# Issuing each dense group of one sequence's projection behind a given matmul of the other's attention

## The chip, the cores and the metric

The kernel runs on one core of a Trainium2 chip. A core has a matrix engine (TensorE, PE in the profile, with its weight loads as PEld), a vector engine (DVE), a scalar engine (ACT), GpSimd (POOL), a synchronisation engine (SP) that here only issues DMAs, and 16 DMA engines. Each engine runs its own program in order; between engines there are semaphores. The metric is the device time of one execution in microseconds.

## The reference

One layer of an encoder is applied, with the same weights, to two sequences: the *prompt* (1024 tokens, number 0 in the code) and the *sample* (512 tokens, number 1), each with 16 learned tokens ahead. The widths are 1024, 64 per head, and 2816 in the feed-forward part.

```python
n = rms_norm(x, g_mix)
proj = n @ w_in                                   # qa ka va | qb kb vb, 18 blocks of 128 columns
qa, ka = rope(rms_norm(qa)), rope(rms_norm(ka))   # group A: 8 query heads, 2 key heads
oa = softmax(qa ka^T * scale) va
qb, kb = rope(qb), rope(kb)                       # group B: 4 heads with two maps each
p = softmax(qb kb^T * scale)
ob = rms_norm((p[0] - lam * p[1]) vb)
h = x + concat(oa, ob) @ w_out
m = rms_norm(h)
h = h + (gelu(conv3(m @ w_gate)) * (m @ w_up)) @ w_down
y = rms_norm(h)[16:]
```

## The kernel before

**Numbers.** Products of float32 are made from two rounded halves of each operand, `hi` and `lo`. `split` (L122) makes them, and `mm3` (L129 to 133) adds three matmuls: hi with hi (L131), lo with hi (L132), hi with lo (L133). `dense` (L136) does this for the eight blocks of 128 input channels, so a *dense group*, one tile of 128 output columns by up to 384 tokens, is 24 matmuls. `load_weight` (L144) fetches a weight tile on ACT's DMA queue and splits it.

**Stages.** `trunk_kernel` (L857) first runs the projection of the sample. Then it runs the attention of the sample together with the projection of the prompt; then the attention of the prompt together with all that is left of the sample (output projection and feed-forward); then the rest of the prompt.

**The projection of the prompt** (`projection`, L165) is a generator. It has three token chunks of 384, 384 and 272 for each weight tile. `keys_a` (L301) does the keys of group A, `values` (L333) a tile of values, with transposes at L346, and `pair` (L277) two tiles of queries or keys, with a normalisation matmul at L257 in group A, the rotation on DVE (L292, L294), the sum on POOL (L297) and stores to DRAM on SP (L272). The order is keys A, values A, queries A, values B, queries A, values B, then the keys, queries and values of B in turn. After each dense group it yields its cost, `24 * cw` in `pair` and `25 * cw` in the other two, cw being the number of tokens: 455,520 in sum. What follows a group (normalisation, transposes, stores) is traced when the generator goes on, in one step with the next group.

**The attention** (`attention`, L391) is a generator too. It loads keys and queries (L414) and values (L434), all on SP. `softmax` (L439) makes the scores of up to 128 queries into `ps_s` (L446, L447; two chunks of keys for the sample, three for the prompt), evicts them on DVE (L450), which gives ps_s free for the next, and exponentiates on ACT (L453). There is one buffer of ps_s. `weighted_v` (L456) transposes the probabilities on PE (L467) into ps_t (two buffers), splits them on ACT and DVE, and multiplies by the values into ps_o (L477 to L482); the last part, 16 keys, is L491. A head of group A is four softmaxes (for the sample; the prompt does that twice, as two blocks), a transpose of the reciprocal sums (L500) and a weighted V. After each four heads of A a small *halo* of 8 queries follows. A head of group B is two blocks for the sample, of two and three query tiles with two softmaxes each. The yielded costs add up to 211,728 for the sample: 15,488 for each head of A, 176 for a halo and 21,868 for a head of B. In the prompt a block of A is 29,824.

**What sets the order.** `merge` (L823) draws from the two generators in turn, by the costs passed so far. This is the order of tracing and the priority in the scheduler, which lays out each engine's program from modelled times: an instruction that is ready may come ahead of one traced earlier that isn't. `tc.issue_after(ins)` adds an edge to every instruction traced inside it on the engine of `ins`: it is placed behind `ins` in that engine's program. For an edge within one engine there is no semaphore.

In the first call, `LEAD1` lets the projection go 20,000 units ahead, and `R1` has it traced at 1.1 units per unit of attention; when the attention is through, `merge` ends, and the rest of the projection is traced by `drain` (L843). `HOLD` places the first four steps of the attention behind the dense group traced before them. In the second call `LEAD2` lets the prompt's attention go 120,000 units ahead, four blocks, and HOLD places the first four steps of the sample's output projection behind the last matmul of weighted V traced by then.

**Memory.** The projection's and the attention's tiles of the prompt lie on the same side of SBUF, one after the other: the prompt's attention gets its tiles as those of the projection are released. PSUM's ps_s, ps_t and ps_o are opened anew for the prompt's attention, in the banks that the sample's held.

```python
        with ExitStack() as es1:
            merge(g, attention(es1, g, 1, "right"), R1[0], p0, R1[1], LEAD1, HOLD)
        drain(p0)
```

Of the kernel before, what the change touches and what calls it, by code (L numbers as in the profile page):

```python
# [21 lines left out]
P = 128  # L22
# [99 lines left out]
def split(g, hi, lo, src, lo_engine=None):  # L122

    nc = g.nc
    return (nc.scalar.copy(hi, src),  # L125
            (lo_engine or nc.vector).tensor_tensor(out=lo, in0=src, in1=hi.bitcast(F32), op=ALU.subtract))  # L126
# [264 lines left out]
def attention(ctx, g, s, side):  # L391
    nc, tc = g.nc, g.tc
# [23 lines left out]
    def load_q(j, maps, c0, cw):  # L416
        out = []
        for first in range(2):
            q = qp.tile([P, max(514, 2 * max(sum(m for _, m in b) for b in blocks))], F32R, name="q", tag=f"q{first}")
            for i, m in enumerate(maps):  # L420
                stacked(q[:, i * cw:(i + 1) * cw], j, m, first, c0, cw)
            out.append(q)
        return out
# [8 lines left out]
    def load_v(i, w, c0):  # L432
        v = vp.tile([P, nf * 2 * P], F32R, name="v", tag="v")[:, :nf * w].rearrange("p (t c) -> p t c", c=w)
        nc.sync.dma_start(out=v.bitcast(F32), in_=g.v[s][0][:, c0 // P] if i == 0 else g.v[s][i])  # L434
        tail = vp.tile([P, P], F32R, name="v_tail", tag="v_tail")[:64 if i == 0 else 96]
        nc.sync.dma_start(out=tail.bitcast(F32), in_=g.vt[s][i][:tail.shape[0], c0:c0 + P])
        return v, tail

    def softmax(q, k, l):  # L439

        M = q[0].shape[-1]
        p = pp.tile([P, ne], F32, name="p", tag="p")[:M]
        ps = g.psum.wide(M, nch, kw)
        for i in range(nch):
            kc = k[:, i * kw:(i + 1) * kw]
            nc.tensor.matmul(ps[:, i], lhsT=q[0], rhs=kc, start=True, stop=False)  # L446
            nc.tensor.matmul(ps[:, i], lhsT=q[1], rhs=kc, start=False, stop=True)  # L447

        nm = sp.tile([P, 1], F32, name="nm", tag="nm")[:M]
        g.evicted = nc.vector.tensor_scalar(out=p.rearrange("p (i w) -> p i w", i=nch), in0=ps, scalar1=-HD ** -0.5,  # L450
                                            scalar2=3.0e38, op0=ALU.mult, op1=ALU.min, accum_out=nm).ins
        p = p[:, :n]
        nc.scalar.activation(p, p, AF.Exp, bias=nm, scale=-1.0, accum_out=l)  # L453
        return p

    def weighted_v(pl, v, diff):  # L456

        W = sum(p.shape[0] for p in pl)
        o = g.psum.tile(P, W, "o")
        v, v_tail = v  # L460

        def transposed(k0, kw):
            tps = g.psum.tile(kw, W, "t")
            c = 0
            for p in pl:
                M = p.shape[0]
                nc.tensor.transpose(tps[:, c:c + M], p[:, k0:k0 + kw], g.ident[:M, :M])  # L467
                c += M
            return tps

        for i in range(nf):
            tps = transposed(i * P, P)
            hi = ptp.tile([P, 512], F32R, name="pt_hi", tag="pt_hi")[:, :W]
            lo = ptp.tile([P, 512], F32R, name="pt_lo", tag="pt_lo")[:, :W]
            split(g, hi, lo, tps)
            if diff:
                nc.tensor.matmul(o, lhsT=v[:, i, 0:P], rhs=hi, start=i == 0, stop=False)  # L477
                nc.tensor.matmul(o, lhsT=v[:, i, P:2 * P], rhs=hi, start=False, stop=False)  # L478
                nc.tensor.matmul(o, lhsT=v[:, i, 0:P], rhs=lo, start=False, stop=False)  # L479
            else:  # L480
                nc.tensor.matmul(o, lhsT=v[:, i, :], rhs=hi, start=i == 0, stop=False)  # L481
                nc.tensor.matmul(o, lhsT=v[:, i, :], rhs=lo, start=False, stop=False)  # L482
            yield 5 * W

        tps = transposed(n - 32, 32)
        parts = ptp.tile([P, 512], F32R, name="pt_hi", tag="pt_hi")[:, :W]
        g.marks = [i.ins for i in split(g, parts[0:32], parts[32:64], tps)]
        if diff:
            nc.scalar.copy(parts[64:96], tps)
        rows = v_tail.shape[0]  # L490
        g.mark = nc.tensor.matmul(o, lhsT=v_tail, rhs=parts[:rows], start=False, stop=True).ins  # L491
        yield 2 * W
        return o, W

# [35 lines left out]
    for kv in range(2):  # L530
        k = load_k(KA, kv)
        v = load_v(0, P, kv * P)
        halo = [sp.tile([P, 8], F32R, name="halo", tag=f"halo{f}", bufs=2) for f in range(2)]
        for i in range(4):
            h = kv * 4 + i
            for b in range(nblk):
                q = load_q(QA + 2 * kv, [i], NMETA + 512 * b - 2, 514)
                load_r()
                pl = []
                l = sp.tile([P, 4], F32, name="l_a", tag="l_a", bufs=3)  # L540
                for t in range(4):
                    pl.append(softmax([x[:, 2 + t * P:2 + (t + 1) * P] for x in q], k, l[:, t:t + 1]))
                    if t == 1 and b == 0:
                        with tc.issue_after(g.evicted):
                            for f in range(2):
                                nc.vector.tensor_copy(halo[f][:, 2 * i:2 * i + 2], q[f][:, 0:2])
                    yield 2 * n
                cols = slice(1 + 512 * b, 513 + 512 * b)
                reciprocals(l, g.rT[s][h, cols].rearrange("(t p) -> t p", p=P))
                o, W = yield from weighted_v(pl, v, False)  # L550
                oa = finish_a(o, W)
                store_a()
                late.append((oa, g.rT[s][h:h + 1, cols], g.oT[s][h * HD:(h + 1) * HD, cols]))
        l = sp.tile([P, 4], F32, name="l_a", tag="l_a", bufs=3)[:8, 0:1]
        load_r()
        p = softmax(halo, k, l)
        r = sp.tile([P, 4], F32, name="r_a", tag="r_a", bufs=3)[:8, 0:1]
        nc.vector.reciprocal(out=r, in_=l)
        nc.scalar.activation(p, p, AF.Copy, scale=r)
        o, W = yield from weighted_v([p], v, False)  # L560
# [34 lines left out]
    for h in range(4):  # L595
        ks = [load_k(KB + h // 2 * 2, h % 2 * 2 + m) for m in range(2)]
        v = load_v(1 + h, 2 * P, 0)
        rows = g.oT[s][512 + h * P:512 + (h + 1) * P]
        for blk in blocks:
            c0 = blk[0][0]  # L600
            W = sum(m for _, m in blk)
            q = load_q(QB + h // 2 * 2, [h % 2 * 2 + m for m in range(2)], c0, W)
# [3 lines left out]
            lead = 1 if c0 < NMETA else 0  # L606
# [213 lines left out]
        yield 4 * cw  # L820


def merge(g, a, wa, b, wb, lead, hold):  # L823

    done = [0.0, lead]
    after, held = None, 0
    while True:
        i = 0 if b is None or done[0] / wa <= done[1] / wb else 1
        if i == (lead > 0) and held < hold:
            after, held = after or g.mark, held + 1  # L830
            order = g.tc.issue_after(after)
        else:
            order = nullcontext()
        try:
            with order:
                done[i] += next((a, b)[i])
        except StopIteration:
            if i == 0:
                break
            b = None  # L840


def drain(gen):  # L843
    for _ in gen:
        pass
# [5 lines left out]
NRAW, NW = 2, 3  # L851
R1, R2 = (1.0, 1.1), (1.0, 1.0)
LEAD1, LEAD2, HOLD, STATS = -20000.0, 120000.0, 4, 26


@with_exitstack
def trunk_kernel(ctx, tc, g):  # L857
    nc = tc.nc
# [73 lines left out]
    with ExitStack() as es0:  # L932
        p0 = projection(es0, g, 0, "left", "mm", "mm")
        with ExitStack() as es:
            zero = zp.tile([16, 2 * P], F32, name="zero")
            nc.vector.memset(zero, 0.0)
            g.zero = zp.tile([16, 2 * P], F32R, name="zero_r")
            nc.vector.tensor_copy(g.zero, zero)
            p1 = projection(es, g, 1, "right", "p", "t")
            for _ in range(STATS):  # L940
                next(p1)
            next(p0)
            drain(p1)
        zes.close()
        g.psum.relay(s=1, t=2, o=1)
        with ExitStack() as es1:
            merge(g, attention(es1, g, 1, "right"), R1[0], p0, R1[1], LEAD1, HOLD)
        drain(p0)
    g.psum.close()
    g.psum = Psum(tc, "psb", mm=2)  # L950
# [1 line left out]
    with ExitStack() as es1:  # L952
        st1 = state(es1, 1, "right", True)

        def sample():
            yield from mixer_out(g, 1, st1, "right", True, "mm")
            yield from conv_glu(es1, g, 1, st1, "right", 1)
        f1 = sample()
        with ExitStack() as es0:
            merge(g, attention(es0, g, 0, "left"), R2[0], f1, R2[1], LEAD2, HOLD)  # L960
        drain(f1)
        g.psum.relay(s=3)
        st0 = state(ctx, 0, "left", False)
        drain(mixer_out(g, 0, st0, "left", False, "s"))
# [69 lines left out]
```

## Time and profile before

| | |
|---|---|
| time, median of 3 runs | 2184.26 us |
| lowest and highest | 2183.82 and 2185.66 us |
| the profiled execution's own time | 2184.81 us |
| its span, first to last instruction | 2182.7 us |
| mean granted TensorE clock | 0.989 |
| PE busy | 2114.2 us (97%) |
| DVE busy | 1319.2 us (60%) |
| ACT busy | 1024.9 us (47%) |
| POOL busy | 624.0 us (29%) |

The profile is that of one execution. Matmuls overlap in the engine's pipeline, so one lasts longer than it holds up the next: the pace is read from the starts. A row of the timeline is start, duration (both in us), engine, line, operation, what it writes and reads, its size, how many were merged into the row, and in brackets the idle time of that engine ahead of it with what ended it. A row of the windows view is a stretch of time, its length, then the busy time with the number of instructions, the granted clock of PE, the mean busy share of the DMA engines and the GB/s that they moved. Some matmul records, a few per cent, can be missing.

### The profile page before, as it was taken

The page shows a single profiled execution, that of the slowest core. Times are in us where ns is not written, and L with a number is a line of the kernel's source. Part 1 is how long each engine was busy: PE and PEld are TensorE (multiplying, and loading weights), DVE is VectorE, ACT ScalarE, POOL GpSimd, SP SyncE. Part 2 cuts the span into 40 slices and gives each one's busy share as a digit, 9 for nine tenths or more (in the row PEclk, how much of TensorE's full clock was granted, in tenths as well). Part 3 has the DMA queues.
Part 4 walks back from the last instruction along what each step waited for, and adds up shares of the span by engine and source line. Part 5 has one row for each costly group of instructions (what it writes and reads, how often), then busy time and mean ns, then how long its engine had stood idle before and what let it go on. Part 6 is the DMA issues. An engine that isn't in the chain of part 4 may idle for free.

```text
span 2182.7 us, 32285 instructions
## 1 busy us (share of the span) xinstructions
PE 2114.2 (97%) x12442; PEld 1899.7 (87%) x12442; DVE 1319.2 (60%) x2288; ACT 1024.9 (47%) x1803; POOL 624.0 (29%) x465
## 2 busy tenths in 40 slices
PE   8999999988999999999999998999999999999997
PEld 7889999986897888898889898988888888888886
DVE  7645565777767667677777766754434344443346
ACT  6434545667756444677777645542121222112224
POOL 5763444310123222344454314530011100111004
PEclk9999999989999999999999999999999999999999
DMA  6663445563233223232332126511111111111112
GB/s 237 214 218 110 149 156 172 162 209 93 76 94 90 88 68 92 90 108 96 110 111 88 65 88 213 183 68 47 41 49 39 58 49 49 44 34 58 49 39 78
DMA packets 112137, 222.77 MB, mean 102 GB/s; under 512 B 14064, under 2 KB 65520, under 8 KB 111472
## 3 DMA queue, kind: packets, MB, share of 16 engines
q1 hardware_dynamic: 83184, 115.84, 16.7%
q10 hardware_dynamic: 28800, 104.87, 14.7%
q8 instruction: 98, 1.61, 0.3%
q14 instruction: 55, 0.45, 0.1%
HBM read 172.11 MB, written 48.55 MB: 101 GB/s over the span
## 4 chain that ended last, share of the span: by engine, by line
PE 82%; DVE 8%; ACT 3%; issue 3%; DMA 2%; POOL 1%; SPq 0%; ACTq 0%; DVEq 0%; POOLq 0%
PE ps_mm L131 20%; PE ps_mm L132 20%; PE ps_mm L133 20%; PE ps_t L467 5%; PE ps_s L446 4%; PE ps_s L447 3%; PE ps_o L482 2%; DVE p L450 1%; PE ps_o L481 1%; PE ps_o L479 1%; DVE w_lo L126 1%; PE ps_o L477 1%; PE ps_o L478 1%; DVE y L797 1%; DVE pt_lo L126 1%
## 5 line engine op out<-in xcount | busy, mean ns | idle before, releaser
L131 PE MATMUL ps_mm<-xhi,w_hi 128*128 128x512 f32 (+6 forms) x2112 | 703.4, 334 | 2.6 <-DVE hn L117 2.5
L133 PE MATMUL ps_mm<-xhi,w_lo 128*128 128x512 f32 (+6 forms) x2112 | 698.1, 331 | 0.0
L132 PE MATMUL ps_mm<-xlo,w_hi 128*128 128x512 f32 (+6 forms) x2112 | 697.9, 331 | 0.0
L131 PEld LDWEIGHTS ps_mm<-xhi,w_hi 128*128 128x128 f32 x2112 | 400.0, 190 | 28.4 <-DVE hn L117 3.1
L132 PEld LDWEIGHTS ps_mm<-xlo,w_hi 128*128 128x128 f32 x2112 | 399.4, 189 | 25.0 <-issue 0.5
L133 PEld LDWEIGHTS ps_mm<-xhi,w_lo 128*128 128x128 f32 x2112 | 399.2, 189 | 24.4 <-issue 0.5
L125 ACT CAST w_hi<-w_f 128x1024 fp32r<-128x1024 f32 x134 | 139.2, 1047 | 389.9 <-PE ps_mm L132 359.4
L126 POOL TENSOR_TENSOR a_lo<-gate,a_hi 128x512 fp32r<-128x512 f32 x66 | 100.7, 1525 | 651.8 <-ACT a_hi L125 651.6
L450 DVE TENSOR_SCALAR_CACHE_REDUCE p<-ps_s 128x1044 f32<-128x1044 f32 (+7 forms) x212 | 223.3, 1053 | 92.8 <-PE ps_s L447 77.1
L125 ACT CAST pt_hi<-ps_t 128x512 fp32r<-128x512 f32 (+8 forms) x360 | 171.0, 484 | 197.2 <-PE ps_t L467 180.3
L771 DVE TENSOR_TENSOR h<-ps_mm,h 128x512 f32<-128x512 f32 (+1 forms) x288 | 182.3, 645 | 123.7 <-PE ps_mm L133 122.8
L453 ACT ACTIVATE p<-p,nm 128x1040 f32<-128x1040 f32 (+7 forms) x212 | 215.3, 1016 | 85.2 <-DVE p L450 84.4
L126 DVE TENSOR_TENSOR pt_lo<-ps_t,pt_hi 128x512 fp32r<-128x512 f32 (+6 forms) x312 | 173.1, 564 | 102.4 <-ACT pt_hi L125 101.4
L131 PE MATMUL ps_mm<-a_hi,w_hi 128*128 128x512 f32 (+1 forms) x576 | 214.6, 384 | 1.2 <-ACT a_hi L125 1.2
L132 PE MATMUL ps_mm<-a_lo,w_hi 128*128 128x512 f32 (+1 forms) x576 | 215.3, 377 | 0.0
L133 PE MATMUL ps_mm<-a_hi,w_lo 128*128 128x512 f32 (+1 forms) x576 | 215.0, 376 | 0.0
L446 PE MATMUL ps_s<-k,q 128*128 128x348 f32 (+6 forms) x552 | 180.2, 332 | 16.5 <-DVE p L450 16.1
L467 PE MATMUL ps_t<-ident,p 128*128 128x128 f32 (+10 forms) x1188 | 183.8, 269 | 0.3 <-ACT r_rows L502 0.3
L447 PE MATMUL ps_s<-k,q 128*128 128x348 f32 (+6 forms) x552 | 173.7, 320 | 0.0
L126 DVE TENSOR_TENSOR w_lo<-w_f,w_hi 128x1024 fp32r<-128x1024 f32 x100 | 123.4, 1243 | 78.0 <-ACT w_hi L125 77.8
L467 PEld LDWEIGHTS ps_t<-ident,p 128*128 128x128 f32 (+10 forms) x1188 | 142.4, 136 | 29.1 <-issue 4.1
L759 DVE TENSOR_TENSOR gate<-ps_mm,gate 128x512 f32<-128x512 f32 x66 | 45.6, 690 | 186.8 <-PE ps_mm L133 184.6
(200 smaller groups left out, 3367.3 us busy)
## 6 DMA issues: line engine op xcount, KB each, us to landing
w_f<-w_gate ACTq DMA_DIRECT2D x44, 512.0 KB, 3.4
w_f<-w_up ACTq DMA_DIRECT2D x44, 512.0 KB, 3.4
w_f<-w_down ACTq DMA_DIRECT2D x44, 512.0 KB, 4.3
w_f<-w_in ACTq DMA_DIRECT2D x36, 512.0 KB, 3.4
w_f<-w_out ACTq DMA_DIRECT2D x32, 512.0 KB, 3.8
q<-qk SPq DMA_DIRECT2D x48, 257.0 KB, 3.8
qk<-hi SPq DMA_DIRECT2D x20, 384.0 KB, 2.5
qk<-hi SPq DMA_DIRECT2D x20, 272.0 KB, 3.2
```

The costliest lines, as they stand in the source:

```text
L125: return (nc.scalar.copy(hi, src), (lo_engine or nc.vector).tensor_tensor(out=lo, in0=src, in1=hi.bitcast(F32), op=ALU.subtract))
L126: (lo_engine or nc.vector).tensor_tensor(out=lo, in0=src, in1=hi.bitcast(F32), op=ALU.subtract))
L131: nc.tensor.matmul(ps, lhsT=whi, rhs=xhi, start=start, stop=False)
L132: nc.tensor.matmul(ps, lhsT=whi, rhs=xlo, start=False, stop=False)
L133: return nc.tensor.matmul(ps, lhsT=wlo, rhs=xhi, start=False, stop=stop).ins
L446: nc.tensor.matmul(ps[:, i], lhsT=q[0], rhs=kc, start=True, stop=False)
L447: nc.tensor.matmul(ps[:, i], lhsT=q[1], rhs=kc, start=False, stop=True)
L450: g.evicted = nc.vector.tensor_scalar(out=p.rearrange("p (i w) -> p i w", i=nch), in0=ps, scalar1=-HD ** -0.5, scalar2=3.0e38, op0=ALU.mul ...
L453: nc.scalar.activation(p, p, AF.Exp, bias=nm, scale=-1.0, accum_out=l)
L467: nc.tensor.transpose(tps[:, c:c + M], p[:, k0:k0 + kw], g.ident[:M, :M])
L759: nc.vector.tensor_tensor(out=a, in0=up, in1=a, op=ALU.mult)
L771: nc.vector.tensor_tensor(out=hs, in0=ps, in1=hs, op=ALU.add)
```

## The change

The generators now note in `g.at` the matmul that ended the attention's latest step: the last score matmul of a softmax, the last product of a step of weighted V, or its tail. `merge` keeps a list of the attention's steps traced so far, each with the costs passed and that matmul. With a pace of (0.52, 6000.0), a step of the projection that begins at `units` is traced inside `issue_after` of the latest attention step that is in the list and whose costs are at most `0.52 * units - 6000`; without such a step it is traced as before. `merge` also goes on when the attention is through, until the projection is, so that the last steps get their edges too. Only the first of the two calls passes a pace.

```diff
@@ softmax
-            nc.tensor.matmul(ps[:, i], lhsT=q[1], rhs=kc, start=False, stop=True)
+            g.at = nc.tensor.matmul(ps[:, i], lhsT=q[1], rhs=kc, start=False, stop=True).ins
@@ weighted_v
-                nc.tensor.matmul(o, lhsT=v[:, i, 0:P], rhs=lo, start=False, stop=False)
+                g.at = nc.tensor.matmul(o, lhsT=v[:, i, 0:P], rhs=lo, start=False, stop=False).ins
...
-                nc.tensor.matmul(o, lhsT=v[:, i, :], rhs=lo, start=False, stop=False)
+                g.at = nc.tensor.matmul(o, lhsT=v[:, i, :], rhs=lo, start=False, stop=False).ins
...
-        g.mark = nc.tensor.matmul(o, lhsT=v_tail, rhs=parts[:rows], start=False, stop=True).ins
+        g.at = g.mark = nc.tensor.matmul(o, lhsT=v_tail, rhs=parts[:rows], start=False, stop=True).ins
@@ merge
-def merge(g, a, wa, b, wb, lead, hold):
+def merge(g, a, wa, b, wb, lead, hold, pace=None):
 
     done = [0.0, lead]
     after, held = None, 0
-    while True:
-        i = 0 if b is None or done[0] / wa <= done[1] / wb else 1
+    passed, units = [], 0.0
+    while a or b:
+        i = 0 if a and (b is None or done[0] / wa <= done[1] / wb) else 1
+        if a is None and pace is None:
+            break
+        order = nullcontext()
         if i == (lead > 0) and held < hold:
             after, held = after or g.mark, held + 1
             order = g.tc.issue_after(after)
-        else:
-            order = nullcontext()
+        elif i and pace:
+            gates = [ins for at, ins in passed if at <= units * pace[0] - pace[1]]
+            if gates:
+                order = g.tc.issue_after(gates[-1])
         try:
             with order:
-                done[i] += next((a, b)[i])
+                step = next((a, b)[i])
+            done[i] += step
+            if i:
+                units += step
+            else:
+                passed.append((done[0], g.at))
         except StopIteration:
             if i == 0:
-                break
-            b = None
+                a = None
+            else:
+                b = None
@@ constants
+PACE = (0.52, 6000.0)
@@ trunk_kernel
-            merge(g, attention(es1, g, 1, "right"), R1[0], p0, R1[1], LEAD1, HOLD)
+            merge(g, attention(es1, g, 1, "right"), R1[0], p0, R1[1], LEAD1, HOLD, PACE)
```

## The prediction

> **What bounds the kernel now.** I read the page's totals first, then the windows of PE around the stage that the change touches, then the rows of single matmuls.
>
> ```profile
> span 2182.7 us, 32285 instructions
> ...
> PE 2114.2 (97%) x12442; PEld 1899.7 (87%) x12442; DVE 1319.2 (60%) x2288; ACT 1024.9 (47%) x1803; POOL 624.0 (29%) x465
> ...
> PE   8999999988999999999999998999999999999997
> ...
> PEclk9999999989999999999999999999999999999999
> ```
>
> TensorE is the engine that limits the kernel; the ninth and tenth slices (437 to 546 us) are a hollow in it, with the clock's one dent. The profiled run took 2184.81 us, 2.1 us more than its span and 0.55 us over the median of 2184.26; the sums below are made against 2184.8.
>
> The windows view of PE (length, busy time with instructions, granted clock, DMA share, GB/s), cut at events that I show next:
>
> ```profile
> 191.60:372.70 181.10, 178.89 (x1132) 1.00 0.46 149
> ...
> 408.50:451.90 43.40, 43.23 (x302) 1.00 0.46 148
> ...
> 465.00:498.00 33.00, 24.61 (x123) 0.75 0.68 224
> 498.00:510.50 12.50, 10.43 (x55) 0.83 0.16 50
> 510.50:575.00 64.50, 57.91 (x328) 1.00 0.31 91
> ```
>
> The same view for L131 alone, the first of the three matmuls of each dense product; eight of them make a dense group:
>
> ```profile
> 158.50:191.60 33.10, 11.83 (x32) 0.90 0.43 115
> 191.60:372.70 181.10, 81.20 (x241) 1.00 0.46 149
> 372.70:383.90 11.20, 4.88 (x15) 1.00 0.56 197
> 383.90:408.50 24.60, 11.52 (x34) 1.00 0.54 164
> 408.50:451.90 43.40, 20.86 (x64) 1.00 0.46 148
> 451.90:465.00 13.10, 7.08 (x23) 1.00 0.51 180
> 465.00:575.00 110.00, 0.00 (x0) 0.91 0.40 126
> ```
>
> Until 465 PE is full; then there is no dense group for 110 us, and in the first 33 of them PE works on 123 matmuls at a clock of 0.75. The work that could have filled this was spent before. The marks are the last matmul of each piece of weighted V (L491, timeline of PE):
>
> ```profile
> 191.57 0.49 PE L491 MATMUL ps_o<-pt_hi,v_tail 64*128 64x512 f32 x1
> ...
> 372.75 0.27 PE L491 MATMUL ps_o<-pt_hi,v_tail 64*128 64x8 f32 x1
> ...
> 408.53 0.30 PE L491 MATMUL ps_o<-pt_hi,v_tail 96*128 96x306 f32 x1
> ...
> 451.89 0.31 PE L491 MATMUL ps_o<-pt_hi,v_tail 96*128 96x306 f32 x1
> ...
> 485.98 0.41 PE L491 MATMUL ps_o<-pt_hi,v_tail 96*128 96x306 f32 x1 [0.53 <-ACT pt_hi L489]
> ...
> 510.48 0.40 PE L491 MATMUL ps_o<-pt_hi,v_tail 96*128 96x306 f32 x1 [0.49 <-ACT pt_hi L489]
> ...
> 531.23 0.50 PE L491 MATMUL ps_o<-pt_hi,v_tail 64*128 64x512 f32 x1
> ...
> 574.73 0.50 PE L491 MATMUL ps_o<-pt_hi,v_tail 64*128 64x512 f32 x1
> ```
>
> The sample's first head of group A ends at 191.6, its whole group A at 372.7, the first, second, third and fourth head of group B at 408.5, 451.9, 486.0 and 510.5. With dense groups a head of B takes 43.4 us (408.5 to 451.9), without them 24.5 (486.0 to 510.5, at a lowered clock and beside the prompt's first softmaxes). From 531.2 the prompt's attention runs alone, a block each 14.5 us, until its fourth ends at 574.7.
>
> **What a unit costs.** Paces come from starts of neighbouring dense matmuls, twelve and three apart; the last row is the last dense matmul of the projection:
>
> ```profile
> 399.68 0.33 PE L131 MATMUL ps_mm<-xhi,w_hi 128*128 128x384 f32 x1
> ...
> 401.76 0.34 PE L131 MATMUL ps_mm<-xhi,w_hi 128*128 128x384 f32 x1
> ...
> 464.07 0.29 PE L131 MATMUL ps_mm<-xhi,w_hi 128*128 128x272 f32 x1
> ...
> 464.45 0.29 PE L131 MATMUL ps_mm<-xhi,w_hi 128*128 128x272 f32 x1
> ...
> 464.91 0.30 PE L133 MATMUL ps_mm<-xhi,w_lo 128*128 128x272 f32 x1
> ```
>
> So 0.173 us for 384 columns and 0.127 for 272; a group of 24 takes 4.15 or 3.05 us. In `merge`'s units a column tile of weights (two groups of 384, one of 272) is 24*1040 = 24,960 and takes 11.35 us: **0.455 us per thousand units**, 1,040 units for each counted L131. The projection has 455,520 units (values and keys of A count 25 instead of 24 per column), the sample's attention 211,728: 15,488 for a head of A, 176 for a halo, 21,868 for a head of B.
>
> **The gate against what ran.** A group that begins at U units may not pass the attention's point 0.52*U - 6000. Turned round, at point A at most (A + 6000)/0.52 may have begun. At the end of the first head (A = 15,488) that is 41.3 thousand; before it was 26 (keys of A) + 32*1.04 = 59.3. At the end of group A (124,256): 250.5 against 59.3 + 241*1.04 = 309.9. After two heads of B (167,992): 334.6 against 309.9 + 113*1.04 = 427.4. The gate binds throughout, the more the later. At the end of attention (211,728) it lets 418.7 begin, so four groups, those from 424,032 on, come behind the last matmul.
>
> **The change part by part.** The edges lie within PE's own program: no instruction is added, no semaphore, and tracing order stays as it was. What a gated step holds back is all of its PE work, also the normalisation's matmul (L257) and the transposes of values (L346) of the group before; its DVE, ACT and POOL work follows the data, its DMA stores move back with it on SP, and the weight loads, which aren't on PE, come no later, so they are hidden as now. Since PE takes its program in order, what is issued behind a gate waits too; the gate's matmul itself waits for softmax on DVE and ACT, and there lies the risk.
>
> *First head.* 18.0 thousand units fewer: 8.2 us, end at 183.4. *Rest of group A.* 250.6 becomes 209.2 thousand, 18.8 us fewer; 181.1 becomes 162.3 and the end 345.7. That supposes PE stays full. It has reason to: the prompt's block with softmaxes twice as wide goes at 14.5 us alone, and a sample's head here still has 22.
>
> *Group B.* A head in company took 43.4 us with 64*1.04 = 66.6 thousand units, 30.3 us of dense and 13.1 of everything else. The gate leaves 21,868/0.52 = 42.05. No row shows a head with that much, so I bound it. If PE stays full (**packed**): 43.4 - 24.55*0.455 = 32.2. If softmax steps come either as full of dense as now or with none (**stitched**, 63% at 43.4 and 37% at 24.5): 36.4. I take the middle, 34.3, since a step that gets a third of a group hides its wait as well as one that gets a whole, and both will occur. The first two heads took 79.2 us after group A instead of 86.8, as their first softmaxes ran before it ended; I keep these 7.6 us. Four heads: attention ends at 345.7 + 4*32.2 - 7.6 = 466.9 packed, 475.3 middle, 483.7 stitched (510.5 before).
>
> *Behind the last matmul.* Four groups, 2*4.15 + 2*3.05 = 14.4 us, nothing beside them, and I add 2 for the two groups before, gated within the last block (0 to 8.3). The last dense matmul, T, then starts at 483, 492 or 500, instead of 464.9.
>
> *The join.* The prompt's attention needs the memory of the projection's tiles, so its loads follow T:
>
> ```profile
> 463.25 2.10 SPq L414 DMA_DIRECT2D k<-ka  x2
> 467.59 2.47 SPq L414 DMA_DIRECT2D q<-qk  x4
> ```
>
> ```profile
> 466.28 1.35 POOL L297 TENSOR_TENSOR y<-y,z 128x544 f32<-128x544 f32 x1 [3.54 <-DVE c L574]
> ```
>
> ```profile
> 498.07 1.25 DVE L450 TENSOR_SCALAR_CACHE_REDUCE p<-ps_s 128x1044 f32<-128x1044 f32 x1 [0.73 <-PE ps_s L447]
> ...
> 507.46 1.25 DVE L450 TENSOR_SCALAR_CACHE_REDUCE p<-ps_s 128x1044 f32<-128x1044 f32 x1 [0.54 <-PE ps_s L447]
> ...
> 510.03 1.25 DVE L450 TENSOR_SCALAR_CACHE_REDUCE p<-ps_s 128x1044 f32<-128x1044 f32 x1 [0.82 <-PE ps_s L447]
> ```
>
> ```profile
> 517.53 0.27 PE L500 MATMUL ps_t<-ident,r_a 128*4 128x128 f32 x1
> ```
>
> ```profile
> q<-qk SPq DMA_DIRECT2D x48, 257.0 KB, 3.8
> ```
>
> The load of q went out 2.7 us after the last dense matmul, and lands 3.8 us later: with the second half, first scores at T + 7.5, an idle PE till then. Before, q was there by 473, and what kept the prompt back was the sample's tail: its first eviction came at 498.1, and the first block, its four softmaxes through by 510, couldn't transpose until 517.5, when the sample had left ps_t. Alone, four softmaxes at 2.57 us and the reciprocal take about 12. From 517.5 to 574.7 four blocks pass, 57.2 us, and this lead without dense work stays as it is, because the second `merge` gets no pace. So the fourth block ends at T + 7.5 + 12 + 57.2 = T + 76.7 instead of 574.7, and **the change pays where T is under 498**. What follows (the sample's output projection and all behind it) begins when this block ends and shifts with it; I cost it at nothing, as neither its order of tracing nor its amounts change, with 3 us either way for another order by chance.
>
> **Sum.** 492 - 498 = -6 us: 2184.8 - 6 = 2179. Packed: 483 - 498 = -15, 2170. Stitched: +2, 2187.
>
> **Rivals.** *Packed*: speaks for it that PE idles only 2.4 us of 224 in the two crowded windows; against it that dense groups come whole there. 2170.
>
> *The heads of B don't get faster* (slower). A head's pace in company may be set by how softmax, eviction and scores follow one another behind a burst of a group, and a burst stays a burst, only rarer. The sum decides at 35.8 us a head; each microsecond above costs four. Half-way from my 34.3 to the old 43.4, at 38.9, T is 510: +12, 2197; at 43.4, it would be 528, +30. For it: 43.4 us under a PE that is full; against it: 24.5 without dense.
>
> *The join costs the clock.* Idle stretches come with a lower clock: 8.4 us idle in the window 465 to 498 with 0.75, then 0.83. The join makes 7.5 idle and 12 nearly so. If softmaxes and first weighted V run at 0.75, PE work of some 4.2 + 12.9 us (24 score matmuls at no more than 0.173, and 90% of a 14.3 us block) takes a third more, 5.7, of which before paid 1 to 2 already: +4, so 2183. [...]
>
> *It does nothing in sum*: what attention gains before T is spent behind it, T between 494 and 502 by stitching, 2181 to 2189.
>
> **How the numbers follow.** This kernel's runs spread by 1.8 us, so no change means within 0.2%, 2179.9 to 2188.6. My forecast (a head of B at 33.3 to 35.3) has 0.40, 0.28 of it faster and 0.12 same; packed 0.20, faster; the clock at the join 0.10 and nothing in sum 0.05, same; slower B 0.25. Faster 0.48, same 0.27, slower 0.25. The range goes from packed with a little more, 2165, to the slower case at 38.9, 2197.
>
> **What would show it.** Right: L491 of the first head near 183, of group A's last halo near 346, of the last head at 467 to 484; dense groups up to T near 492 and a clock of 1.0 until there; first eviction of the prompt 8 us behind T; the fourth block's end near 569. Wrong: idle PE before scores within group A or B with dense groups still gated; heads of B over 36; a join longer than 20 us from T to the first transposes; or a stage from 575 on that has other lengths than now.

## The result, and the profile after

The changed kernel takes 2210.46 us (median of 4 runs, 2208.27 to 2215.32), the kernel before beside it 2184.04: a ratio of 1.0123, interval 1.0111 to 1.0136. It is 26 us **slower**, where 5 us faster had been forecast, and it lies beyond the range, which ended at 2197. The profiled execution took 2212.31 us, its span is 2210.1.

The page of the changed kernel, with the rows that answer to those of before:

```profile
span 2210.1 us, 32272 instructions
...
PE 2121.5 (96%) x12442; PEld 1905.7 (86%) x12442; DVE 1315.0 (59%) x2288; ACT 1020.5 (46%) x1803; POOL 622.1 (28%) x465
...
PE   8899999996999999999999999999999999999997
...
PEclk9999999997999999999999999999999999999999
```

The hollow did not go. It moved into one slice, the tenth (497 to 552 us), and became deeper: PE is at 6 there, where the ninth and tenth were at 8 before, and the clock at 7, where its lowest was 8. The marks that the prediction named stand in the timeline of PE: the ends of the first head, of group A, of the first and last head of group B, the last dense matmul, the prompt's first scores, its first transposes, and the end of its fourth block.

```profile
191.04 0.50 PE L491 MATMUL ps_o<-pt_hi,v_tail 64*128 64x512 f32 x1
...
353.75 0.37 PE L491 MATMUL ps_o<-pt_hi,v_tail 64*128 64x8 f32 x1
...
389.98 0.30 PE L491 MATMUL ps_o<-pt_hi,v_tail 96*128 96x306 f32 x1
...
498.64 0.30 PE L491 MATMUL ps_o<-pt_hi,v_tail 96*128 96x306 f32 x1
...
513.62 0.29 PE L133 MATMUL ps_mm<-xhi,w_lo 128*128 128x272 f32 x1
...
528.07 0.63 PE L446 MATMUL ps_s<-k,q 128*128 128x348 f32 x1 [14.16 <-DMA q<-qk]
...
544.16 0.41 PE L500 MATMUL ps_t<-ident,r_a 128*4 128x128 f32 x1
...
604.50 0.49 PE L491 MATMUL ps_o<-pt_hi,v_tail 64*128 64x512 f32 x1
```

The sample's attention does end earlier, at 498.6 instead of 510.5. But the last dense matmul comes at 513.6 instead of 464.9, the prompt starts 14.5 us behind it, and its fourth block, behind which the sample's output projection begins, ends at 604.5 instead of 574.7: 29.8 us later. From there to the end of the span it is 1605.6 us (1608.0 before). The whole loss lies ahead of this point. The windows view of PE shows how it comes about:

```profile
158.50:191.00 32.50, 27.59 (x156) 0.86 0.39 110
191.00:353.70 162.70, 159.33 (x996) 0.98 0.46 147
353.70:390.00 36.30, 34.10 (x215) 0.93 0.44 139
390.00:426.80 36.80, 35.33 (x243) 1.00 0.56 176
426.80:463.30 36.50, 31.52 (x195) 0.91 0.27 85
463.30:498.60 35.30, 32.96 (x201) 0.95 0.25 85
498.60:513.90 15.30, 15.30 (x101) 1.00 0.59 186
513.90:528.10 14.20, 0.04 (x2) 0.68 1.05 388
528.10:544.20 16.10, 10.64 (x31) 0.50 0.64 219
544.20:604.50 60.30, 56.07 (x326) 0.98 0.17 51
```

Group A takes 162.7 us instead of 181.1, and a head of B about 36 instead of 43.4, with PE idle 1.5 to 5 us in each. Then come the four groups behind the attention, 14.2 us in which PE does nothing while the DMA engines are full (share 1.05, 388 GB/s), and 16.1 us of softmaxes at a granted clock of 0.50.

### The profile page after: what moved, and what is told of

Read it like the earlier page. It is cut to its first block, busy times and chain, and to the rows that moved or that the text cites. A ratio compares the mean times of both kernels' runs of the same rounds, so it can differ in the third digit from the quotient of the medians.

```text
span 2210.1 us, 32272 instructions
## 1 busy us (share of the span) xinstructions
PE 2121.5 (96%) x12442; PEld 1905.7 (86%) x12442; DVE 1315.0 (59%) x2288; ACT 1020.5 (46%) x1803; POOL 622.1 (28%) x465
## 3 DMA queue, kind: packets, MB, share of 16 engines
q1 hardware_dynamic: 83184, 115.84, 16.4%
q10 hardware_dynamic: 28800, 104.87, 14.5%
## 4 chain that ended last, share of the span: by engine, by line
PE 80%; DVE 9%; issue 3%; DMA 3%; ACT 3%; POOL 2%; SPq 0%; ACTq 0%; DVEq 0%; POOLq 0%
PE ps_mm L132 20%; PE ps_mm L131 20%; PE ps_mm L133 20%; PE ps_t L467 5%; PE ps_s L446 3%; PE ps_s L447 3%; PE ps_o L482 2%; DVE p L450 2%; PE ps_o L481 1%; DVE y L797 1%; PE ps_o L479 1%; DMA yT<-y 1%; PE ps_o L478 1%; PE ps_o L477 1%; ACT p L453 1%
## 5 line engine op out<-in xcount | busy, mean ns | idle before, releaser
L131 PE MATMUL ps_mm<-xhi,w_hi 128*128 128x512 f32 (+6 forms) x2112 | 704.1, 334 | 2.6 <-DVE hn L117 2.5
L131 PEld LDWEIGHTS ps_mm<-xhi,w_hi 128*128 128x128 f32 x2112 | 401.6, 190 | 27.7 <-DVE hn L117 3.1
L131 PE MATMUL ps_mm<-a_hi,w_hi 128*128 128x512 f32 (+1 forms) x576 | 215.5, 386 | 1.2 <-ACT a_hi L125 1.2
```

The costliest lines, as they stand in the source:

```text
L131: nc.tensor.matmul(ps, lhsT=whi, rhs=xhi, start=start, stop=False)
```

## The experiments

Two theories. **J**, the join: the prompt's attention can't start before the projection's tiles are released, so the last dense matmul opens it; the change moves this matmul behind the sample's attention, where nothing is left to run beside the loads that follow. **S**, the spreading: dense groups handed out over the attention cover its waits worse than groups that run as they can, and the loss arises within the attention.

I call E the start of the last matmul of the sample's attention, T that of the last dense matmul, F that of the fourth block's end (L491). All times are microseconds; the rest is the span less F. Marks and rest are those of the one profiled execution, the time is the median of all: the executions of the changed kernel alone differ by 7 us.

| kernel | E | T | first scores | F | rest | time, median | ratio to before, interval |
|---|---|---|---|---|---|---|---|
| before | 510.5 | 464.9 | 495.9 | 574.7 | 1608.0 | 2184.04 | |
| changed | 498.6 | 513.6 | 528.1 | 604.5 | 1605.6 | 2210.46 | 1.0111 to 1.0136 |
| cap_a | 506.6 | 483.1 | 494.7 | 571.9 | 1604.6 | 2181.91 | 0.998 to 0.9999 |
| slope46 | 506.5 | 496.4 | 508.9 | 585.7 | 1608.6 | 2194.26 | 1.0034 to 1.0064 |
| tail_only | 498.7 | 513.8 | 529.1 | 605.8 | 1608.8 | 2213.80 | 1.0122 to 1.0153 |
| tail_one | 500.0 | 503.1 | 514.7 | 591.3 | 1607.4 | 2201.08 | 1.0067 to 1.0097 |
| q_first | 499.3 | 514.3 | 527.8 | 604.6 | 1608.0 | 2214.04 | 1.0128 to 1.0156 |
| warm | 498.5 | 513.5 | 532.0 | 605.9 | 1608.8 | 2215.24 | 1.0132 to 1.016 |
| q_free | 495.3 | 510.3 | 520.6 | 597.3 | 1612.0 | 2212.15 | 1.0118 to 1.0152 |
| cap_a_q | 508.2 | 484.7 | 496.9 | 573.5 | 1606.0 | 2181.31 | 0.9985 to 1.0002 |

### The gate only up to the end of group A (cap_a)

```diff
-            gates = [ins for at, ins in passed if at <= units * pace[0] - pace[1]]
+            gates = [ins for at, ins in passed if at <= min(units * pace[0] - pace[1], 124256.0)]
```

> The gate never passes the end of the sample's group A, so in group B dense groups are as free as in the kernel before. Theory J (the projection's last dense matmul opens the prompt's attention, and the change moves it 49 us back and leaves nothing to run beside the loads behind it): the last dense matmul at about 481, one head of B alone behind it, which covers the loads; the prompt's fourth block ends near 568 and the time is about 2177, 7 under the kernel before. Theory S (spreading dense groups thins steps of attention to their own pace, wherever it is done): nothing won in group A either, 2184 to 2190.

Measured: T 483.1, F 571.9, 2181.91 us. The marks are 2 and 4 us later than J expected, the time 5 us longer. The time can hardly be told from that of the kernel before (its interval ends at 0.9999). So 18 us more of T cost nothing here: the sample's tail still stood behind it, and F comes 65.3 us behind E, before 64.2. It also comes 88.8 us behind T, so the two are about level in this run.

### A flatter pace (slope46)

```diff
-PACE = (0.52, 6000.0)
+PACE = (0.46, 6000.0)
```

> Pace 0.46 instead of 0.52: at the end of attention 473 thousand units may have begun, all of the projection, so no groups are left behind the last matmul. J: time follows the last dense matmul, which comes some 12 us earlier than with 0.52: about 2198. S: the heads of B at about 38 us each instead of 36, so attention ends later by as much as the end is spared: 2206 to 2211.

Measured 2194.26 us, even less than J's 2198. E is the same as in cap_a within 0.1 us, T is 13.3 later and F 13.8. With E fixed, F follows T one for one, and the time nearly so (12.4 us).

### Dense work of the sample in the join (after_fill, before_fill)

```diff
-            merge(g, attention(es0, g, 0, "left"), R2[0], f1, R2[1], LEAD2, HOLD)
+            merge(g, attention(es0, g, 0, "left"), R2[0], f1, R2[1], 0.0, 0)
```

> The changed kernel with the lead of the prompt's attention over the sample's output projection taken from 120,000 units to 0, and the hold with it: dense groups of the output projection may run in the join and beside the prompt's first four blocks. J: the idle join and the half clock go; 20 to 30 us less than the changed kernel, 2180 to 2190. S: the loss lies ahead of the join, and what is won here is no more than in the same edit of the kernel before.

> The same edit of the lead and hold in the kernel before, as control. Here the sample's tail covers the join, and the lead of four blocks has 64.5 us with 57.9 busy. J and S: up to 8 us less, 2176 to 2184; J: it wins far less than the same edit on the changed kernel.

Measured 2215.35 us for the changed kernel with this edit (1.0144, 1.0129 to 1.016) and 2206.22 for the kernel before with it (1.01, 1.0085 to 1.0115). Neither of the expected times came (J's 2180 to 2190 is missed by 25 us), and the edit costs the kernel before 22 us. Most of that shows at the other end of the prompt's attention: from 1250 to 1450 us PE idles 23.5 us in before_fill, 7.8 in the kernel before. L131 in the windows view of the kernel before,

```profile
1250.00:1300.00 50.00, 21.97 (x64) 1.00 0.22 71
1300.00:1330.00 30.00, 14.29 (x43) 0.89 0.60 211
```

and of before_fill:

```profile
1250.00:1300.00 50.00, 7.63 (x27) 0.97 0.10 32
1300.00:1330.00 30.00, 0.94 (x2) 0.84 0.19 66
```

What is spent early isn't there from 1250 on, 27 and 2 dense products instead of 64 and 43. The comparison that the two runs were made for still stands: with the join filled, the changed kernel is 9 us behind its control, without it 26. By this comparison about 17 of the 26 us are idle time that other work can take; from 500 to 560 us PE is busy for 53.2 us in after_fill, for 39.3 in the changed kernel.

### Only the tail (tail_only, tail_one)

The decisive pair. No group is spread; in the first only the last four dense groups are issued behind the attention, in the second only the last one.

```diff
-            gates = [ins for at, ins in passed if at <= units * pace[0] - pace[1]]
+            gates = [ins for at, ins in passed] if units >= 424032.0 else []
```

(448992.0 in tail_one)

> Only the last four dense groups of the projection are gated, behind the attention's last traced matmul; all groups before are as free as in the kernel before. Theory J, with the rule that the first runs gave (the prompt's fourth block ends at the later of 65 us behind the last matmul of the sample's attention and 89 us behind the last dense matmul): that attention ends about 503, as 14 us of dense are out of its way; the last dense matmul at about 518, the fourth block's end at about 607, the time about 2216, slower than the fully paced kernel, though no group is spread. Theory S (the loss comes of spreading groups over the attention): 14 us of dense moved to the end, at most 8 over the kernel before, 2184 to 2192.

> Only the very last dense group of the projection (24 matmuls of 272 columns, 3 us) is gated, behind the attention's last traced matmul; all others are free. Theory J with its rule (the prompt's fourth block ends at the later of 65 us behind the attention's last matmul and 89 us behind the last dense matmul): attention ends at 507 to 508, the last dense matmul at about 512, the fourth block at about 601, the time about 2210: 3 us of work in the wrong place cost 26. If instead the amount of dense work left behind the attention decides, a fourth group's share of the loss of tail_only: about 2191.

tail_only takes 2213.80 us. Its marks, from the timeline of PE:

```profile
498.65 0.41 PE L491 MATMUL ps_o<-pt_hi,v_tail 96*128 96x306 f32 x1 [0.64 <-ACT pt_hi L489]
...
513.78 0.29 PE L133 MATMUL ps_mm<-xhi,w_lo 128*128 128x272 f32 x1
...
605.83 0.49 PE L491 MATMUL ps_o<-pt_hi,v_tail 64*128 64x512 f32 x1
```

These are the marks of the changed kernel to within 0.2 us for E and T. So the whole loss is in the last four groups, and the spreading of all the others does nothing to the end of the attention, neither for nor against it (that E agrees to 0.01 us is chance: idle time and clock differ on the way). S falls. So does what I had counted as gain: both kernels do the same PE work before 498.6, and both leave nearly the same idle time, the one in a lump after the projection, the other a little in each head. PE's window of tail_only, 16 us idle; the first six rows of the changed kernel's windows above add up to 320.8 busy of 340.1, 19 idle:

```profile
158.50:498.60 340.10, 323.72 (x1994) 0.93 0.43 136
```

tail_one shows how little it takes: one group of 3 us behind the attention costs 18 us (2201.08). This time lies midway between the two expected, 2210 and 2191; but it is well over a fourth of tail_only's loss of 30.5 us, and the marks decide. F is 88.1 us behind T, as J's rule has it; what J had wrong was the end of the attention, 500.0 and not 507. The likely cause, not tested by itself, is that the prompt's first softmaxes (from 498 in the kernel before) no longer ran beside its last block. With T 503.1 instead of 512, F came 10 us sooner than expected. This run also shows what the loads wait for. From 496 to 512 us the loads of the prompt's keys (L414) and values (L434) waited on SP for dense matmuls (us in total, times, longest):

```profile
SPq L414 <- PE ps_mm L133: 5.6, 1, 5.6
...
SPq L434 <- PE ps_mm L133: 1.4, 1, 1.4
```

### What the join is made of (q_first, q_free, warm, cap_a_q)

q_first takes the loads of the sample's mixed heads behind the prompt's first queries:

```diff
...
+                if s == 0 and g.qload is None and first == 1:
+                    g.qload = d.ins
...
+                        with g.tc.issue_after(g.qload) if s == 1 else nullcontext():
+                            nc.sync.dma_start(out=h[:, k, c0:c0 + cw], in_=g.oT[s][k * P:(k + 1) * P, c0:c0 + cw])
```

> The changed kernel with the eight loads of the sample's mixed heads (2 MB) issued behind the prompt's first load of queries. If the join's 14.5 us, where 7.5 were reckoned, come of transfers sharing the DMA engines and of the order on SP's queue, the join falls to 8 to 10 us and the time by 4 to 6, to 2205. If the memory's release sets it, nothing changes: 2210.

The join fell from 14.4 to 13.5 us only, and the time did not fall at all. SP's timeline in the changed kernel shows why 2 MB less ahead help little:

```profile
515.27 1.25 SPq L414 DMA_DIRECT2D k<-ka  x2
517.00 0.52 SPq L434 DMA_DIRECT2D v<-v  x1
518.59 1.00 SPq L272 DMA_DIRECT2D qk<-hi  x2
519.88 0.36 SPq L272 DMA_DIRECT2D qk<-y  x1
520.94 0.49 SPq L436 DMA_DIRECT2D v_tail<-vt  x1
523.12 2.77 SPq L414 DMA_DIRECT2D q<-qk  x4
```

The prompt's queries go out 9.5 us behind T, last in a row that holds the stores of the projection's last chunk, which wait for ACT (1.4 us) and POOL (0.5 us; waits of SP, 510 to 535 us), and the values. That is no news of the change. The row q<-qk at 467.59, from which the prediction took its 2.7 us, is the load of the *sample's* last queries: a block of 306 queries, 153 KB a load. The prompt's loads, 514 queries or 257 KB each, are the next of that name. The DMA view of the kernel before, from 467.0 to 470.2 us and from 474.2 to 476.9 us, tells them apart by size:

```profile
q<-qk SPq DMA_DIRECT2D x4, 153.0 KB
...
q<-qk SPq DMA_DIRECT2D x4, 257.0 KB, 5.6
```

The second stands last in the same row of loads and stores (timeline of SP, before):

```profile
471.28 0.50 SPq L272 DMA_DIRECT2D qk<-hi  x1
471.83 1.31 SPq L434 DMA_DIRECT2D v<-v  x1
473.30 0.96 SPq L436 DMA_DIRECT2D v_tail<-vt  x1
474.30 2.54 SPq L414 DMA_DIRECT2D q<-qk  x4
```

474.3 is 9.4 us behind the last dense matmul of 464.9. The join was in the trace of before, at its full length, under the sample's tail. q_free takes things out of that row:

```diff
+        out = nc.scalar if s == 0 and dst is g.qk[0][5] and c0 > 700 else nc.sync
...
+        early = load_q(QA, [0], NMETA - 2, 514) if s == 0 and kv == 0 else None
```

> The changed kernel with three things taken from ahead of the prompt's first queries on SP's queue: the stores of the projection's last chunk (issued by ACT instead), the first load of values (traced after the queries) and the loads of the sample's mixed heads. If the order on SP made the join 14.5 us instead of 7.5, first scores come 8 to 10 us behind the last dense matmul and the time is 4 to 6 under the changed kernel, 2204 to 2206; if the DMA engines' load sets it, the join stays at 12 or more, with 2208 to 2211.

The join is 10.3 us, so the order on SP is worth 4 of its 14.4. The traces show what the rest is made of. In the changed kernel the queries go out 9.5 us behind T, and the first scores follow 5.0 later; in q_first it is 7.0 and 6.5, in q_free 3.6 and 6.7. In the first two the DMA engines are full meanwhile: a share of 1.07 in the changed kernel from 523.0 to 528.1 us, of 1.03 and 1.06 in q_first from 515 to 525 and from 525 to 535 us. What the order saves is lost in part to a longer transfer; no run shows what would shorten that. F came 7.2 us sooner, 3.3 of it because the attention itself ended sooner. The time didn't: 2212.15, as the rest of the kernel took 1612.0 instead of 1605.6. Of these 6.4 us 4.0 arise between some 732 and 897 us behind F; why is not shown. Over all runs this rest lies between 1604.6 and 1612.0; effects under some 5 us can't be shown in the time of this kernel by such edits, only in the marks.

warm adds matmuls on constants in the join; it does more work than the kernel, and writes a result that nothing reads.

```diff
+    with tc.issue_after(g.mark):
+        spare = g.psum.tile(P, 372, "mm")
+        for _ in range(28):
+            nc.tensor.matmul(spare, lhsT=g.ones_d, rhs=g.vec[:, :372], start=True, stop=True)
```

> The changed kernel with 28 float32 matmuls of 372 columns on constants added behind the last dense matmul, whose result nobody reads: they keep PE busy for some 11 us of the 14.5 us join. If the clock that the idle join costs makes the four softmaxes 3.46 us each instead of 2.57, these come back to 2.6 and the time falls by 4 to 7, to 2205; if the clock has no part in it, nothing or a little more.

They took 17 us instead of 11 and held the first scores up until 532.0, so the time could not fall. But they show the clock's price. The granted clock is 1.00 in warm from 515 to 535 us, 0.50 in the changed kernel from 525 to 545; of the six score matmuls of the first softmax, the later ones start 0.16 us apart in warm and 0.29 in the changed kernel. Evictions of the first softmaxes (timeline of DVE) in warm,

```profile
533.45 1.25 DVE L450 TENSOR_SCALAR_CACHE_REDUCE p<-ps_s 128x1044 f32<-128x1044 f32 x1 [16.36 <-PE ps_s L447]
...
536.00 1.25 DVE L450 TENSOR_SCALAR_CACHE_REDUCE p<-ps_s 128x1044 f32<-128x1044 f32 x1 [1.30 <-PE ps_s L447]
```

and in the changed kernel:

```profile
537.49 1.25 DVE L450 TENSOR_SCALAR_CACHE_REDUCE p<-ps_s 128x1044 f32<-128x1044 f32 x1 [2.05 <-PE ps_s L447]
...
540.95 1.25 DVE L450 TENSOR_SCALAR_CACHE_REDUCE p<-ps_s 128x1044 f32<-128x1044 f32 x1 [2.20 <-PE ps_s L447]
```

2.55 us from one to the next on a PE that had been busy, 3.46 on one that had been idle. Starting 3.9 us later, warm has its first transposes (545.2) only 1.1 later, so the clock is worth 2.8 us of this stretch here. It does not stay up: between softmaxes PE waits for DVE, 1.34 to 1.42 us each time, the granted clock is 0.70 from 535 to 545 us, score matmuls start 0.29 us apart from 540.4 us on, and warm's own step from the third eviction (538.58) to the fourth (542.04) takes 3.46 again.

cap_a_q joins cap_a and q_first:

> The gate capped at the end of group A, as cap_a, together with the loads behind the first queries. J: with the last dense matmul at about 483 both terms of the rule stood level at 572; the join shortens by 4 to 6, but the other term, 65 us behind the attention's end, stays, so 0 to 2 us under cap_a, 2180 to 2182. If the join alone set the end there, 2176.

Measured 2181.31 us: no difference from cap_a, as J expected. No version beat the kernel before by more than 0.1%.

## Why the prediction was wrong

Two steps failed, and each alone would have turned the sign: T, forecast at 492 and measured at 513.6, mostly by the heads of group B, and the one called *The join*: "the change pays where T is under 498". Where T comes too late for the sample's tail to cover it, F is 88.1 to 92.5 us behind T (tail_one, slope46, q_first, the changed kernel, tail_only, warm; 87.0 in q_free), not 76.7. So the point where it pays is near 485, and by this alone my own T of 492 would have given a kernel some 6 us slower. Two of the prediction's own signs of being wrong came true: heads of B over 36 us (36.2), and more than 20 us from T to the first transposes (30.5).

- *The bound.* Right: PE has a hollow for want of dense work. Wrong is what I made of it. The hollow of the kernel before paid for something: during it the prompt's tiles were released, its loads landed, and its first softmaxes ran. There E sets the end (F = E + 64), and T could come 18 to 20 us later for nothing, as cap_a and cap_a_q show. The prediction named the loads that the tail covered, but priced them at 7.5 us.
- *First head.* 183.4 forecast, 191.0 measured: a term of 7.6 us mis-sized. The gate held back less than the 18.0 thousand units reckoned, which are 17 of the 32 L131s counted before; 29 are still there. All four softmaxes of the second head stand in PE's program ahead of the first head's last product at 191.04, so the attention's point there is not 15,488 but 15,488 + 4*1,056 = 19,712, and 49.4 thousand units may have begun, not 41.3. And PE idles 4.9 of the 32.5 us at a clock of 0.86, not much more than before (3.9, 0.89). The view of L131 and the timeline of PE in the changed kernel:

```profile
158.50:191.00 32.50, 9.56 (x29) 0.86 0.39 110
```

```profile
169.87 0.59 PE L446 MATMUL ps_s<-k,q 128*128 128x264 f32 x1 [0.81 <-DVE p L450]
...
172.69 0.57 PE L446 MATMUL ps_s<-k,q 128*128 128x264 f32 x1
...
180.28 0.36 PE L446 MATMUL ps_s<-k,q 128*128 128x264 f32 x1
...
190.32 0.29 PE L446 MATMUL ps_s<-k,q 128*128 128x264 f32 x1
```

- *Rest of group A.* 162.3 forecast, 162.7 measured. Right.
- *Group B.* 34.3 us a head forecast, 36.2 measured (353.7 to 498.6, by four): the case called stitched, at 36.4. And the 7.6 us that its first softmaxes saved beside group A weren't saved again. Together 15.3 us mis-sized.
- *Behind the last matmul.* 16.4 forecast, 15.0 measured. Right.
- *T* was therefore 492 forecast, 513.6 measured: 21.6 of the 35.8 us by which F missed my 568.7.
- *The join* makes the other 14.2: the loads 14.45 instead of 7.5 us (the misread row is 6.8 of these 6.95: 9.5 instead of 2.7), the four softmaxes to the first transposes 16.1 instead of 12, the four blocks 60.3 instead of 57.2, all of it in the first (16.8 instead of 13.7; the other three take 43.5 in both).
- *What follows F* costs nothing: right, 1605.6 against 1608.0.
- *The rivals.* The slower one had the right sign and point (it decides from 35.8 us a head, measured 36.2), but a head never came to 38.9; heads got faster, and what decided was elsewhere. The join's clock I held for 4 us and no change. The softmaxes of the join ran at a clock of 0.50 (528.1 to 544.2), behind 14.2 idle us; the stretch took 4.1 us more than my 12, of which warm shows 2.8 to be the clock's.

The deeper fault is in the sum's form. I compared one instant, T, with the time at which the prompt had started before, as if the time were T plus a constant in both kernels. The runs agree with a maximum of two terms, E + 65 and T + 89; before it was the first, after it is the second, and the change traded 12 us of the first for 49 of the second. The second term rests on seven runs; the first on the kernel before, and on cap_a and cap_a_q, where both are level.

## What to carry to other kernels

Filler work that runs out early isn't wasted if its end opens the next stage: look what its last instruction releases (memory, loads) before it is moved back. "Both end together" leaves the start of the next stage bare; let the one that holds the next stage's memory end first, by as much as the next stage needs to load, here some 24 us (89 - 65). And moving filler within a stretch may only move its idle time: between tail_only and the changed kernel it did no more than that.

## What the runs showed of the hardware

Two programs of quite another order, all groups spread and none, reach E at 498.64 and 498.65 and T at 513.62 and 513.78. A float32 matmul of 372 columns held PE for 0.62 us at a granted clock of 1.00 (28 of them in 17.3 us, 56 records in the trace of warm), while one of 384 columns in the rounded type held it for 0.173 in the kernel before (twelve starts from 399.68 to 401.76 us, clock 1.00), so the filler of 28 was longer than reckoned, 17.3 us for 11. And a chain of softmaxes that left PE idle for 1.3 to 1.4 us in each step of 2.6 did not keep the clock that it found: in warm the granted clock was 1.00 from 525 to 535 us and 0.70 from 535 to 545, and score matmuls that started 0.16 us apart when it began did so 0.29 apart some 8 us later.
